# A hybrid decoder layer on one core: the conv layer norm, the first attention head, the second FFN norm and the seam of the FFN's two phases rearranged

## The chip, the cores and the metric

The kernel runs on one core of a Trainium2 chip. The core has TensorE (PE; its weight loads are shown as PEld), VectorE (DVE), ScalarE (ACT), GpSimd (POOL) and SyncE (SP), which issues nearly all DMA transfers here. The metric is the device time of one execution in microseconds (us).

## The reference

One decoder layer is computed for 1024 prompt tokens and for 8 sequences of 4 new tokens over 2048 cached positions, 1056 tokens in all, in float32:

- `h = rmsnorm(x) @ w_in`, split into a convolution input, latent queries, latent keys, a rotary key and two gates.
- Convolution branch: `u = a * sigmoid(g)`, a depthwise convolution of width 31 over 512 channels, then `y = silu(_layernorm(y, ln_g, ln_b))` with `_layernorm = (y - mean) * rsqrt(mean((y - mean)^2) + 1e-6) * g + b`, and `y @ w_conv_out`.
- Attention: 8 heads of 96 features, of which 32 are rotary; q and k of each head are RMS-normalised (`_head_norm`) before causal softmax attention. The sample tokens attend to a paged cache.
- `x = x + (sigmoid(g_conv) * conv + sigmoid(g_mla) * mla) @ w_out`, and at last the FFN, `x = x + (silu(h2 @ w_gate) * (h2 @ w_up)) @ w_down` with `h2 = rmsnorm(x)`, 1024 model features and 2816 hidden ones.

## The kernel before

**Arithmetic.** Each float32 operand of a large matmul is split into a rounded high part and a rest (`split`, L75 and L76: a cast on ACT, a subtraction on DVE or POOL), and each product takes three matmuls: high times high, rest times high, high times rest. Nearly all of them are recorded at L70.

**Conv layer norm.** The 1056 tokens are handled in three thirds `q` of 352 columns. `ln_mm` sums over the channels with a matmul by ones, `ln_b` subtracts the mean and squares, and `ln_c` (L416 to L431) works out `1/sqrt(v + eps)` as a full tile of 128 x 352: sqrt on ACT, reciprocal on DVE, one correction step. Then it multiplies `y`, applies silu (four channel blocks, L430) and splits the result into `cvh` and `cvl`, the operand of the `w_conv_out` product. Meanwhile PE computes the gates, `g()`: matmuls whose result ACT reads with a sigmoid into `sgo` (L345). Mean and variance are hung behind single gate tiles by `then=`.

**Attention.** Token blocks 0 to 7 get q and k (`qn`, `kn`) by `d_norm`, `d_post`. In `d_post` a block is multiplied by its reciprocal roots `r`: `qn` on DVE (L640), `kn` on POOL in two pieces (L644 and L646; the second piece of block 7 on DVE). Then the heads begin: `e_prep` transposes qn and kn of four blocks, splits them (qh, kh on ACT; ql, kl on DVE), and `e_score` makes a row block of scores in PSUM (`ps__...`, two banks), which DVE masks and minimises in one custom operation into `sm` (L867). The mask is set up by POOL (L786 to L788) and by ACT (L789).

**FFN norm.** The RMS norm of the last token block (`norm_a` to `norm_d`, L1460 to L1551) stands in line with the first FFN products, which `eight` and `go` place.

**FFN.** Both phases use seven products instead of eight (Strassen's scheme in 2 x 2 blocks; `ORDER` and `DORD` list the seven). Phase 1 has 11 strips `g`; each has a unit for the gate and one for the up projection (`unit`, L1725). A unit is 7 products x 2 column halves x 12 matmuls of 264 columns. The seven combinations of a finished strip go to DRAM (`td`, stores at L1637); `d_load` and `d_sums` read the strip's part of `w_down`, form four combinations on POOL and DVE and store them (`sd`, L1626 to L1634). Phase 2 has 14 rounds of 11 steps; a step is 12 matmuls and needs a right operand of `td` (`d_b`: load L1775, cast L1781, subtraction L1782) and, every second step, a strip of `w_down` or `sd` (`d_w`: load L1798 or L1800, cast L1810, subtraction L1811). Loads run four pieces ahead; there are three buffers for a split strip and 28 slots for right operands.

**What sets the order.** Each engine works through its instructions in the order of the program, after a scheduler with priorities (`tc.high_priority`) has placed them. SP issues the DMAs in order, too: a store that waits for its data holds up every load that stands behind it.

Of the kernel before, what the change touches and what calls it, by code (L numbers as in the profile page):

```python
# [44 lines left out]
def build(tc, a, o, upto="Z", dbg=None):  # L45
# [369 lines left out]

    def ln_c(q):  # L416
# [50 lines left out]
    g()  # L467
    w_c = [wload(wp, a["w_conv_out"][0, :, 0:2 * P], 4, 2 * P, G)]
# [19 lines left out]
    vhl = qkv.tile([P, 8, H, 2, DV], F32R, name="vhl")  # L488
    dq = pool("dq", side="right")
# [101 lines left out]
    def d_qk(i):  # L591
# [5 lines left out]
        if i < 8:  # L597
# [23 lines left out]
    def d_stats(j):  # L621
# [12 lines left out]
        V.scalar_tensor_tensor(out=r, in0=t, scalar=1.5, in1=r, op0=ALU.add, op1=ALU.mult)  # L634

    def d_post(i):
# [9 lines left out]
        (V if i == 7 else G).tensor_tensor(out=kn[:, i, :, DN:], in0=pe_all[:, i, :].unsqueeze(1).to_broadcast([P, H, DR]),  # L646
# [100 lines left out]
    d_post(6)  # L747
    d_post(7)
# [104 lines left out]
    def e_score(h, i):  # L853
# [4 lines left out]
        for g_ in range(i // 4 + 1):  # L858
# [8 lines left out]
        V.tensor_tensor_reduce(out=sm[:, :n], in0=ps_[:, :n], in1=mask[:, NP_ - n:], scale=1.0, scalar=BIG,  # L867
                               op0=ALU.add, op1=ALU.min, accum_out=st[:, 0:1])
# [839 lines left out]
    def unit(u, nxt, order):  # L1708
        for n_ in order:
# [7 lines left out]
            if u[0] == "u":  # L1717
# [47 lines left out]

    def d_b(n):

        for _ in range(n):
            if len(DB) == len(dbs):
                return  # L1770
            while len(dbt) < min(len(DB) + 4, len(dbs)):
                xi, k = dbs[len(dbt)]
                ts = [ctile(F32) for _ in range(2)]
                for q in range(2):
                    SP.dma_start(ts[q], td[DORD[xi] - 1, k, :, q * CQ:(q + 1) * CQ])  # L1775
                dbt.append(ts)
            x = dbs[len(DB)]
            hi, lo = slots[len(DB) % len(slots)]
# [8 lines left out]

    def d_w(n):

        while len(dwo) <= min(n, len(dws) - 1):  # L1790
            while len(dwr) < min(len(dwo) + 4, len(dws)):
                xi, p, kp = dws[len(dwr)]
                x, m = DORD[xi], min(2, NF2 - 2 * kp)
                w = rawtile()[:, 0:m * 2 * P]
                if x in (1, 2, 4):
                    j, i = {1: (0, 0), 2: (1, 0), 4: (1, 1)}[x]
                    c0 = (4 * i + 2 * p) * P
                    SP.dma_start(w.rearrange("p (e c) -> p e c", e=m), wdv[:, j, 2 * kp:2 * kp + m, c0:c0 + 2 * P])  # L1798
# [6 lines left out]
            if n_ >= len(dws) - 6:  # L1805

# [126 lines left out]
```

## Time and profile before

| | us |
|---|---|
| three runs | 1828.26, 1828.10, 1824.87; median 1828.1 |
| profiled execution | 1829.26 |
| its span (first to last instruction) | 1827.5 |
| PE busy in it | 1759.0 (96%) |
| DVE, ACT, POOL busy | 1252.3, 841.7, 769.8 |
| mean granted TensorE clock | 0.987 of full |

The span is the part of the execution that the profiler's records cover. An engine's busy share is an average over stages; the waits say which engine's work another one stood still for, and the windows give busy time, instruction counts, granted TensorE clock and DMA rate of a stretch.

### The profile page before, as it was taken

The page shows a single profiled execution, that of the slowest core. Times are in us where ns is not written, and L with a number is a line of the kernel's source. Part 1 is how long each engine was busy: PE and PEld are TensorE (multiplying, and loading weights), DVE is VectorE, ACT ScalarE, POOL GpSimd, SP SyncE. Part 2 cuts the span into 40 slices and gives each one's busy share as a digit, 9 for nine tenths or more (in the row PEclk, how much of TensorE's full clock was granted, in tenths as well). Part 3 has the DMA queues.
Part 4 walks back from the last instruction along what each step waited for, and adds up shares of the span by engine and source line. Part 5 has one row for each costly group of instructions (what it writes and reads, how often), then busy time and mean ns, then how long its engine had stood idle before and what let it go on. Part 6 is the DMA issues. An engine that isn't in the chain of part 4 may idle for free.

```text
span 1827.5 us, 34749 instructions
## 1 busy us (share of the span) xinstructions
PE 1759.0 (96%) x12932; PEld 1708.2 (93%) x12932; DVE 1252.3 (69%) x2437; ACT 841.7 (46%) x1892; POOL 769.8 (42%) x855
## 2 busy tenths in 40 slices
PE   8999999999899999999989999999999999799999
PEld 8999999989788899999979999999999999799998
DVE  5329999746788867666758689767676666666433
ACT  5311122554588867777763145332333333455332
POOL 2212112125655634343322047756555555665431
PEclk9999999999899999999999999999999999899999
DMA  6211222254000022121245210454445444887432
GB/s 209 63 52 48 71 84 94 82 178 123 1 30 12 2 88 70 59 82 53 93 146 174 82 30 27 145 152 150 149 154 161 140 145 148 250 247 232 146 96 93
DMA packets 197156, 199.15 MB, mean 109 GB/s; under 512 B 17400, under 2 KB 180516, under 8 KB 194931
## 3 DMA queue, kind: packets, MB, share of 16 engines
q1 hardware_dynamic: 194043, 178.05, 31.2%
q0 software_dynamic: 2944, 18.88, 3.1%
q8 instruction: 102, 1.67, 0.4%
q14 instruction: 67, 0.55, 0.1%
HBM read 145.87 MB, written 51.42 MB: 108 GB/s over the span
## 4 chain that ended last, share of the span: by engine, by line
PE 75%; DVE 9%; ACT 7%; DMA 3%; issue 3%; POOL 1%; SPq 1%; DVEq 0%; ACTq 0%; POOLq 0%
PE ps L70 51%; PE pp L70 6%; PE pd L70 3%; PE po L1117 2%; PE pq L70 2%; PE pt L891 1%; DMA c<-td 1%; PE ptc L1023 1%; PE po L905 1%; ACT pr L870 1%; ACT sqf L1043 1%; DVE b L1491 1%; PE pt L70 1%; PE pk L70 1%; DVE sm L867 1%
## 5 line engine op out<-in xcount | busy, mean ns | idle before, releaser
L70 PE MATMUL ps<-b,wh 128*128 128x264 f32 x3544 | 655.5, 287 | 14.3 <-ACT wh L1810 10.4
L70 PEld LDWEIGHTS ps<-b,wh 128*128 128x128 f32 x3544 | 552.9, 190 | 15.3 <-ACT wh L1810 10.7
L70 PE MATMUL ps<-b,wl 128*128 128x264 f32 x1772 | 503.9, 286 | 3.9 <-DVE wl L1811 3.0
L70 PEld LDWEIGHTS ps<-b,wl 128*128 128x128 f32 x1772 | 335.1, 190 | 5.5 <-DVE wl L1811 3.9
L1348 ACT CAST wh<-wr 128x512 fp32r<-128x512 f32 x157 | 97.1, 619 | 219.3 <-PE ps L70 180.4
L70 PE MATMUL ps<-hTh,wh 128*128 128x352 f32 x552 | 179.9, 326 | 0.0
L70 PE MATMUL ps<-hTl,wh 128*128 128x352 f32 x552 | 178.1, 323 | 0.0
L70 PE MATMUL ps<-hTh,wl 128*128 128x352 f32 x552 | 178.0, 322 | 0.0
L70 PE MATMUL pp<-panh,cTh 128*128 128x272 f32 x512 | 157.0, 307 | 8.0 <-DVE sraw L1044 6.5
L357 DVE SCALAR_TENSOR_TENSOR y<-up,cw,y 128x1024 f32<-128x1024 f32 x120 | 158.0, 1362 | 0.7
L986 POOL TENSOR_TENSOR cNl<-craw,cNh 128x256 fp32r<-128x256 f32 x128 | 88.7, 694 | 165.1 <-ACT cNh L985 165.0
L1349 POOL TENSOR_TENSOR wl<-wr,wh 128x512 fp32r<-128x512 f32 x78 | 105.3, 1350 | 110.3 <-ACT wh L1348 78.1
L70 PE MATMUL pp<-panh,cTl 128*128 128x272 f32 x512 | 149.2, 291 | 0.0
L70 PE MATMUL pp<-panl,cTh 128*128 128x272 f32 x512 | 147.8, 289 | 0.0
L70 PEld LDWEIGHTS pp<-panh,cTh 128*128 128x128 f32 x512 | 96.4, 188 | 12.3 <-DVE sraw L1044 10.2
L70 PEld LDWEIGHTS ps<-hTh,wh 128*128 128x128 f32 x552 | 103.7, 188 | 0.7
L70 PEld LDWEIGHTS ps<-hTl,wh 128*128 128x128 f32 x552 | 103.7, 188 | 0.6
L70 PEld LDWEIGHTS ps<-hTh,wl 128*128 128x128 f32 x552 | 103.7, 188 | 0.0
L872 POOL TENSOR_TENSOR pr<-pr,ste 128x128 f32<-128x128 f32 (+3 forms) x64 | 73.2, 1147 | 60.0 <-DVE ste L871 34.5
L76 POOL TENSOR_TENSOR wl<-wr,wh 128x1024 fp32r<-128x1024 f32 x13 | 37.7, 2902 | 142.2 <-ACT wh L75 142.2
L70 PEld LDWEIGHTS pp<-panl,cTh 128*128 128x128 f32 x512 | 96.9, 189 | 0.0
L1043 ACT ACTIVATE sqf<-pp 128x512 f32<-128x512 f32 x128 | 76.4, 597 | 44.2 <-ACT cTh L75 28.9
(888 smaller groups left out, 4361.5 us busy)
## 6 DMA issues: line engine op xcount, KB each, us to landing
td<-c SPq DMA_DIRECT2D x154, 132.0 KB
c<-td SPq DMA_DIRECT2D x154, 132.0 KB
wr<-in_w_in SPq DMA_DIRECT2D x24, 512.0 KB
wr<-in_w_gate SPq DMA_DIRECT2D x44, 256.0 KB
wr<-in_w_up SPq DMA_DIRECT2D x44, 256.0 KB
c<-in_w_down SPq DMA_DIRECT2D x88, 128.0 KB
sd<-c SPq DMA_DIRECT2D x88, 128.0 KB
wr<-sd SPq DMA_DIRECT2D x40, 256.0 KB
```

What stands on the lines that cost most here:

```text
L70: TE.matmul(out, l, r, start=first and i == 0, stop=last and i == n - 1)
L76: (eng or V).tensor_tensor(out=lo, in0=src, in1=f(hi), op=ALU.subtract)
L357: V.scalar_tensor_tensor(out=y[:, c, 0:NP_], in0=up[:, j:j + NP_], scalar=cw[:, c, j:j + 1], in1=y[:, c, 0:NP_], op0=ALU.mult, op1=ALU.add)
L867: V.tensor_tensor_reduce(out=sm[:, :n], in0=ps_[:, :n], in1=mask[:, NP_ - n:], scale=1.0, scalar=BIG, op0=ALU.add, op1=ALU.min, accum_out= ...
L870: at["ACT"] = S.activation(pr[:, :n], sm[:, :n], AF.Exp, scale=-1.0, bias=st[:, 0:1], accum_out=st[:, 1:2]).ins
L872: at["POOL"] = G.tensor_tensor(out=pr[:, :n], in0=pr[:, :n], in1=st[:, 2:3].to_broadcast([P, n]), op=ALU.mult).ins
L891: TE.transpose(pt[:, j, :], pr[:, (j0 + j) * P:(j0 + j + 1) * P], ident)
L986: G.tensor_tensor(out=nl[:, j], in0=craw[:, j], in1=f(nh[:, j, 0:KL]), op=ALU.subtract)
L1043: s["at"] = S.activation(sq, pp[:, :, wc], AF.Square).ins
L1117: TE.matmul(d, l, r, start=(pg == 0 and z == 0), stop=(pg == NPG and z == 1))
L1348: S.copy(h_, src[u][x][:, c])
L1349: eng.tensor_tensor(out=l_, in0=src[u][x][:, c], in1=f(h_), op=ALU.subtract)
```

## The change

- Conv layer norm: the variance is summed as 4 x 88 tokens on partitions (four matmuls by two columns of ones), its root is a power on POOL over 88 x 4 numbers, a copy on DVE spreads it over 128 columns, and four transposes on PE bring it back as rows. Silu becomes `z * sigmoid(z)`: sigmoid on ACT, `z` and the product on DVE. `ln_c` of a third is hung behind the next gate tile, and the split is made in halves. The split of the first `w_conv_out` strip moves from POOL to DVE.
- Attention: for blocks 6 and 7 the multiplications by the reciprocal roots move from before the first head to behind the first `sm`, in one 128 x 768 piece for kn as for qn. The reciprocal roots are kept in `csT`. The wide part of the mask is set after the operands of the first head.
- FFN norm: `norm_b(3)` moves behind two more `go`/`eight` pieces, `d_load(0, 0)` behind `norm_d(2, ...)`.
- FFN seam: in the last strip (`g` = 10) `d_load` and `d_sums` move from the up unit to the gate unit. The loads of the first five right operands are issued before the last unit (`d_bl(5)`), those of the first strips inside it (`d_wl`), and loading is separated from splitting. Split strips get nine buffers in place of three (six of the slots), right operands 22 slots in place of 28. In phase 2 strips are loaded eight ahead and split four ahead.

The core of the diff:

```diff
+    def ln_var(q):
+
+        pv = psb.tile([P, 512], F32, tag="s", name="ps", bufs=8)
+        for j in range(4):
+            TE.matmul(pv[:SUB, 2 * j:2 * j + 2], lns[q][:, j * SUB:(j + 1) * SUB], ones[:, 0:2], start=True, stop=True)
+        st = pb.tile([SUB, 2, 4], F32, tag="lnst", name="lnst", bufs=2)
+        V.tensor_scalar(out=st[:, 0], in0=pv[:SUB, 0:8].rearrange("p (j z) -> p j z", z=2)[:, :, 0], scalar1=EPS, scalar2=None, op0=ALU.add)
+        G.tensor_tensor(out=st[:, 1], in0=st[:, 0], in1=nhalf[:SUB, 0:4], op=ALU.pow)
+        lnp[q] = pb.tile([SUB, 4, P], F32, tag="lnrb", name="lnrb", bufs=1)
+        V.tensor_copy(lnp[q], st[:, 1].unsqueeze(2).to_broadcast([SUB, 4, P]))
+
     def ln_c(q):
         cs = slice(q * CH, (q + 1) * CH)
-        v = pb.tile([P, CH], F32, tag="sg", name="sg", bufs=2)
-        V.tensor_scalar(out=v, in0=lnp[q][:, :CH], scalar1=EPS, scalar2=None, op0=ALU.add)
-        r = pb.tile([P, CH], F32, tag="rq_r", name="rq_r", bufs=1)
-        t = pb.tile([P, CH], F32, tag="rq_t", name="rq_t", bufs=1)
-        S.activation(t, v, AF.Sqrt)
-        V.reciprocal(r, t)
-        V.tensor_tensor(t, r, r, ALU.mult)
-        V.tensor_tensor(t, t, v, ALU.mult)
-        V.tensor_scalar(out=t, in0=t, scalar1=-0.5, scalar2=1.5, op0=ALU.mult, op1=ALU.add)
-        V.tensor_tensor(r, r, t, ALU.mult)
-        V.tensor_tensor(y[:, :, cs], y[:, :, cs], r.unsqueeze(1).to_broadcast([P, 4, CH]), ALU.mult)
-        for c in range(4):
-            S.activation(y[:, c, cs], y[:, c, cs], AF.Silu, scale=gsm[:, 4 + c:5 + c], bias=gsm[:, 8 + c:9 + c])
-        split(cvh[:, :, cs], cvl[:, :, cs], y[:, :, cs])
+        pr = psb.tile([P, 512], F32, tag="s", name="ps", bufs=8)
+        for j in range(4):
+            TE.transpose(pr[:, j * SUB:(j + 1) * SUB], lnp[q][:, j], ident[:SUB, :SUB])
+        V.tensor_tensor(y[:, :, cs], y[:, :, cs], pr[:, :CH].unsqueeze(1).to_broadcast([P, 4, CH]), ALU.mult)
+
+        for c2 in range(2):
+            sz = pb.tile([P, 2, CH], F32, tag="up", name="sz", bufs=2)
+            for c in (2 * c2, 2 * c2 + 1):
+                g_, b_ = gsm[:, 4 + c:5 + c], gsm[:, 8 + c:9 + c]
+                S.activation(sz[:, c % 2], y[:, c, cs], AF.Sigmoid, scale=g_, bias=b_)
+                V.tensor_scalar(out=y[:, c, cs], in0=y[:, c, cs], scalar1=g_, scalar2=b_, op0=ALU.mult, op1=ALU.add)
+            ys = y[:, 2 * c2:2 * c2 + 2, cs]
+            V.tensor_tensor(ys, ys, sz, ALU.mult)
+            split(cvh[:, 2 * c2:2 * c2 + 2, cs], cvl[:, 2 * c2:2 * c2 + 2, cs], ys)
...
     def var(q):
-        ln_mm(q)
-        ln_c(q)
+        ln_var(q)
+        if q:
+            ln_c(q - 1)
 
     g(then=mean)
     g(then=var)
-    g()
-    w_c = [wload(wp, a["w_conv_out"][0, :, 0:2 * P], 4, 2 * P, G)]
+    g(then=lambda q: q == 0 and ln_c(2))
+    w_c = [wload(wp, a["w_conv_out"][0, :, 0:2 * P], 4, 2 * P)]
...
+            if i > 5:
+                G.tensor_copy(kn[:, i, :, DN:], pe_all[:, i, :].unsqueeze(1).to_broadcast([P, H, DR]))
...
+        S.activation(mask[:, 0:NP_ - P].rearrange("p (j q) -> p j q", j=7), ident.unsqueeze(1).to_broadcast([P, 7, P]), AF.Copy, scale=0.0)
         for n_ in range(AH):
             e_score(*flat[n_])
+        at0 = at["DVE"]
+        for i in (6, 7):
+            for eng, t, w in ((V, qn, 0), (G, kn, 1)):
+                with tc.issue_after(at0):
+                    eng.tensor_tensor(out=t[:, i], in0=t[:, i], in1=rr3[:, w, i % 2].unsqueeze(2).to_broadcast([P, H, DH]), op=ALU.mult)
...
-            if u[0] == "u":
+            if nxt is None:
+
+                d_b({1: 2, 6: 4, 2: 5, 7: 5, 5: 7, 4: 7, 3: 7}[n_])
+                if n_ == 7:
+                    d_bl(7, tmp)
+                d_wl({7: 2, 5: 4, 4: 6}.get(n_, 0))
+                d_w({4: 1, 3: 2}.get(n_, 0))
+            elif u == ("g", NF2 - 1):
+                if n_ in (1, 6):
+                    d_load(u[1], n_ // 6)
+                if n_ in (2, 7):
+                    d_sums(u[1], n_ // 7)
+            elif u[0] == "u":
                 if n_ in (2, 4):
                     d_load(u[1], n_ // 4)
                 if n_ in (5, 3):
                     d_sums(u[1], (5, 3).index(n_))
-            if nxt is None:
-                d_b(2 if n_ != 3 else 1)
...
     norm_b(3)
-    go(nc_, 1)
-    for x in ((1,), (2,)):
-        for q in range(2):
-            eight(q, 1, x)
+    for q in range(2):
+        eight(q, 1, (2,))
...
+    def d_bl(n, get=lambda: ctile(F32)):
+
+        while len(dbt) < min(n, len(dbs)):
+            xi, k = dbs[len(dbt)]
+            ts = [get() for _ in range(2)]
+            for q in range(2):
+                SP.dma_start(ts[q], td[DORD[xi] - 1, k, :, q * CQ:(q + 1) * CQ])
+            dbt.append(ts)
...
+        while len(DB) < min(n, len(dbs)):
+            x, ts = dbs[len(DB)], dbt[len(DB)]
+            hi, lo = slots[len(DB) % 22]
...
-            if n_ >= len(dws) - 6:
-
-                hi, lo = [t[:, 0:m] for t in slots[(7 * NF2 + n_ - len(dws) + 6) % len(slots)]]
-            else:
-                hi, lo = [t[:, 0:m] for t in whl()]
+            hi, lo = [t[:, 0:m] for t in (whl() if n_ % 9 < 3 else slots[22 + n_ % 9 - 3])]
...
+        if g_ + 1 == NF2:
+            d_bl(5)
         unit(("u", g_), ("g", g_ + 1) if g_ + 1 < NF2 else None, ORDER)
...
+                d_wl(len(dws))
...
-                d_w(6 * t + k // 2 + 2)
-                if (11 * p + k) % 2 == 0 and (xi or p or k > 2):
-                    d_b(1)
+                n_ = 6 * t + k // 2
+                d_wl(n_ + 8)
+                d_w(n_ + 4)
+                n_ = 11 * xi + (11 * p + k) // 2 + 8
+                d_bl(n_ + 4)
+                d_b(n_)
```

The order of the instructions moves as follows. The first place is SP's queue at the end of phase 1: `td` stores are those of a strip's combinations, `wr<-in_w_down` are strips for phase 2, `c<-td` right operands for it. Before (these stand behind the last strip's results):

```order
L1637 DMA td_74<-c_18855 128x264
L1637 DMA td_74<-c_18976 128x264
L1634 DMA sd_75<-c_19325 128x256
L1634 DMA sd_75<-c_19329 128x256
L1634 DMA sd_75<-c_19331 128x256
L1634 DMA sd_75<-c_19327 128x256
L1775 DMA c_19403<-td_74 128x264
L1775 DMA c_19404<-td_74 128x264
L1798 DMA wr_19425<-in_w_down 128x2x256
L1798 DMA wr_19431<-in_w_down 128x2x256
L1798 DMA wr_19437<-in_w_down 128x256
```

After (the `td` stores here are those of strip 9; the ones of strip 10 begin 16 rows below the last one shown; line numbers in rows of after are those of the changed kernel):

```order
L1659 DMA td_74<-c_18439 128x264
L1659 DMA td_74<-c_18455 128x264
L1322 DMA wr_18919<-in_w_up 128x4x128
L1831 DMA wr_19262<-in_w_down 128x2x256
L1831 DMA wr_19264<-in_w_down 128x2x256
L1805 DMA u2_12372<-td_74 128x264
L1805 DMA u3_12373<-td_74 128x264
L1831 DMA wr_19312<-in_w_down 128x2x256
L1805 DMA c_19086<-td_74 128x264
L1805 DMA c_19087<-td_74 128x264
L1805 DMA c_19090<-td_74 128x264
```

The last load of `in_w_up` and the first strips and right operands now stand together, ahead of all stores of strip 10. Before, the fourth to sixth strip stood behind them and behind the `sd` stores.

The second place is POOL at the start of attention, where the mask and kn of blocks 6 and 7 meet. Before:

```order
L644 TENSOR_TENSOR kn_3520<-kn_3520,std_4485 128x8x64
L646 TENSOR_TENSOR kn_3520<-pe_all_82,std_4485 128x8x32
L644 TENSOR_TENSOR kn_3520<-kn_3520,std_4485 128x8x64
L787 MEMSET mask_4667 128x128
L882 MEMSET PTh_4772 128x128
L883 MEMSET PTl_4773 128x128
L788 AFFINE_SELECT mask_4667<-mask_4667 128x128
```

After:

```order
L803 MEMSET mask_4702 128x128
L940 TENSOR_TENSOR kn_3559<-kn_3559,csT_67 128x768 x2
L898 MEMSET PTh_4811 128x128
L899 MEMSET PTl_4812 128x128
L804 AFFINE_SELECT mask_4702<-mask_4702 128x128
```

The copies of the rotary part of kn are made earlier; two multiplications of 128 x 768 stand between the mask's two instructions. On DVE, at the same place, before:

```order
L640 TENSOR_TENSOR qn_3519<-qn_3519,std_4485 128x768 x2
L646 TENSOR_TENSOR kn_3520<-pe_all_82,std_4485 128x8x32
L848 SCALAR_TENSOR_TENSOR ql_4674<-pt_4675,gqT_68,qh_4673 96x512
L76 TENSOR_TENSOR kl_4683<-pt_4684,kh_4682 96x512
L867 ISA sm_4696,ste_4695<-ps__4691,mask_4667 128x128
```

After:

```order
L652 SCALAR_TENSOR_TENSOR csT_67<-std_4524 128x32
L863 SCALAR_TENSOR_TENSOR ql_4708<-pt_4709,gqT_68,qh_4707 96x512
L76 TENSOR_TENSOR kl_4717<-pt_4718,kh_4716 96x512
L882 ISA sm_4731,ste_4730<-ps__4726,mask_4702 128x128
L882 ISA ste_4730 128x1
L940 TENSOR_TENSOR qn_3558<-qn_3558,csT_67 128x768 x2
L882 ISA sm_4742,ste_4741<-ps__4737,mask_4702 128x256
```

ql and kl of the first head come directly behind the reciprocal roots (`csT`), and the two multiplications of qn stand between the first `sm` and the second.

The third place is ACT at the end of the conv layer norm (third `q` = 2). Before:

```order
L75 CAST wh_3420<-wr_3418 128x1024
L345 ACT_TABLE_LOAD
L345 ACTIVATE sgo_3338<-ps_3391 128x352
L345 ACTIVATE sgo_3424<-ps_3425 128x352
L430 ACT_TABLE_LOAD
L430 ACTIVATE y_1203<-y_1203,gsm_65 128x352 x4
L75 CAST cvh_1195<-y_1203 128x4x352
L345 ACT_TABLE_LOAD
L345 ACTIVATE sgo_3424<-ps_3451 128x352
```

After:

```order
L440 ACTIVATE sz_3388<-y_1203,gsm_65 128x352 x2
L75 CAST cvh_1195<-y_1203 128x2x352
L440 ACTIVATE sz_3396<-y_1203,gsm_65 128x352 x2
L75 CAST wh_3459<-wr_3457 128x1024
L345 ACTIVATE sgo_3355<-ps_3430 128x352
L75 CAST cvh_1195<-y_1203 128x2x352
L345 ACTIVATE sgo_3463<-ps_3464 128x352
L75 CAST cvh_1195<-y_1203 128x2x352
L345 ACTIVATE sgo_3463<-ps_3490 128x352
```

The table loads are gone; sigmoids, halves of the cast and gate reads follow each other.

## Rows read from the trace of the kernel before

**Rows 1.** The page: busy time, share of the span, instructions

```profile
PE 1759.0 (96%) x12932; PEld 1708.2 (93%) x12932; DVE 1252.3 (69%) x2437; ACT 841.7 (46%) x1892; POOL 769.8 (42%) x855
```

**Rows 2.** PE's waits: us in total, times, longest

```profile
PE ps L70 <- ACT wh L1810: 10.4, 1, 10.4
...
PE ps L70 <- ACT sgo L345: 4.4, 1, 4.4
...
PE ps L70 <- DVE b L1551: 3.2, 1, 3.2
PE ps__4691 L863 <- DVE kl L76: 3.1, 1, 3.1
PE ps L70 <- DVE wl L1811: 3.0, 2, 1.9
PE ps L1469 <- DVE u L1460: 2.9, 2, 2.6
```

**Rows 3.** The page: DMA issues, KB each

```profile
c<-td SPq DMA_DIRECT2D x154, 132.0 KB
...
wr<-sd SPq DMA_DIRECT2D x40, 256.0 KB
```

**Rows 4.** Phase 2, windows: us, PE PEld DVE ACT POOL busy (x), PEclk, DMA share, GB/s

```profile
1590.00:1594.00 4.00, 2.39 (x11) 2.39 (x12) 0.89 (x1) 1.54 (x3) 2.64 (x3) 0.50 0.95 295
1594.00:1597.00 3.00, 3.00 (x24) 3.00 (x24) 0.87 (x2) 1.60 (x4) 1.31 (x3) 0.90 1.10 360
1629.00:1632.00 3.00, 3.00 (x16) 3.00 (x15) 2.26 (x5) 0.54 (x2) 1.32 (x2) 0.50 0.89 255
1760.00:1780.00 20.00, 20.00 (x168) 20.00 (x167) 6.66 (x15) 4.66 (x9) 3.70 (x4) 1.00 0.36 99
```

**Rows 5.** SP's queue ahead of PE's longest stop: start, us, work

```profile
1578.87 5.40 SPq L1637 DMA_DIRECT2D td<-c  x8
1584.33 1.91 SPq L1634 DMA_DIRECT2D sd<-c  x4
...
1587.27 2.44 SPq L1798 DMA_DIRECT2D wr<-in_w_down  x5
```

**Rows 6.** Windows at the end of the conv norm, columns as in rows 4

```profile
382.50:390.00 7.50, 6.32 (x22) 6.33 (x23) 2.30 (x5) 4.15 (x10) 2.36 (x1) 0.54 0.43 150
390.00:412.00 22.00, 22.00 (x141) 22.00 (x140) 8.08 (x19) 6.29 (x14) 7.77 (x7) 1.00 0.85 271
```

**Rows 7.** ACT ahead of the gate that PE waits for, timeline

```profile
378.06 2.40 ACT L430 ACTIVATE y<-y,gsm 128x352 f32<-128x352 f32 x4 [1.62 <-DVE y L428]
380.48 1.36 ACT L75 CAST cvh<-y 128x1408 fp32r<-128x1408 f32 x1
381.87 1.28 ACT L345 ACT_TABLE_LOAD   x1
```

**Rows 8.** ACT over the conv norm, groups by line

```profile
L345 ACT ACT_TABLE_LOAD x6 | 7.7, 1283 | 0.1
```

**Rows 9.** POOL in the last FFN norm: the power, group by line

```profile
L1472 POOL TENSOR_TENSOR nst<-nst,nhalf 88x3 f32<-88x3 f32 x1 | 1.0, 1039 | 0.0
```

**Rows 10.** DVE at the first head, timeline

```profile
491.32 2.67 DVE L640 TENSOR_TENSOR qn<-qn,std 128x768 f32<-128x768 f32 x2
...
495.34 0.67 DVE L76 TENSOR_TENSOR kl<-pt,kh 96x512 fp32r<-96x512 f32 x1
496.91 0.29 DVE L867 CUSTOM_DVE_ANT_0 sm<-ps__4691,mask 128x128 f32<-128x128 f32 x1 [0.90 <-PE ps__4691 L864]
```

**Rows 11.** POOL at the first head, timeline

```profile
491.37 1.81 POOL L644 TENSOR_TENSOR kn<-kn,std 128x512 f32<-128x512 f32 x1 [1.92 <-DVE std L634]
...
494.44 1.22 POOL L644 TENSOR_TENSOR kn<-kn,std 128x512 f32<-128x512 f32 x1
...
496.05 0.29 POOL L788 TENSOR_SCALAR_AFFINE_SELECT mask<-mask 128x128 f32<-128x128 f32 x1
```

**Rows 12.** Window in the last FFN norm, columns as in rows 4

```profile
1152.50:1155.00 2.50, 0.15 (x1) 0.15 (x1) 2.50 (x5) 0.93 (x2) 2.50 (x3) 0.86 0.32 105
```

More of the change, by code (lines that the diff above doesn't have):

```diff
@@ L414, in ln_b @@
         ln_add(q, [sqa[:, 0], sqa[:, 1], sqb[:, 0], sqb[:, 1]])
+    SUB = 88
+    def ln_var(q):
[7 more added lines that the diff above has]
+        V.tensor_copy(lnp[q], st[:, 1].unsqueeze(2).to_broadcast([SUB, 4, P]))
@@ L488, in build @@
     vhl = qkv.tile([P, 8, H, 2, DV], F32R, name="vhl")
+    rr3 = csT[:, 0].rearrange("p (w z h) -> p w z h", w=2, z=2)
     dq = pool("dq", side="right")
@@ L633, in d_stats @@
         V.tensor_tensor(t, t, v, ALU.mult)
-        V.scalar_tensor_tensor(out=r, in0=t, scalar=1.5, in1=r, op0=ALU.add, op1=ALU.mult)
+        V.scalar_tensor_tensor(out=rr3 if j == 3 else r, in0=t, scalar=1.5, in1=r, op0=ALU.add, op1=ALU.mult)
     def d_post(i):
@@ L645, in d_post @@
                         in1=r[1].unsqueeze(2).to_broadcast([P, H, DN]), op=ALU.mult)
-        (V if i == 7 else G).tensor_tensor(out=kn[:, i, :, DN:], in0=pe_all[:, i, :].unsqueeze(1).to_broadcast([P, H, DR]),
+        G.tensor_tensor(out=kn[:, i, :, DN:], in0=pe_all[:, i, :].unsqueeze(1).to_broadcast([P, H, DR]),
                         in1=r[1].unsqueeze(2).to_broadcast([P, H, DR]), op=ALU.mult)
@@ L866, in e_score @@
         sm = pe_.tile([P, NP_], F32, tag="sm", name="sm", bufs=2)
-        V.tensor_tensor_reduce(out=sm[:, :n], in0=ps_[:, :n], in1=mask[:, NP_ - n:], scale=1.0, scalar=BIG,
-                               op0=ALU.add, op1=ALU.min, accum_out=st[:, 0:1])
+        x = V.tensor_tensor_reduce(out=sm[:, :n], in0=ps_[:, :n], in1=mask[:, NP_ - n:], scale=1.0, scalar=BIG,
+                                   op0=ALU.add, op1=ALU.min, accum_out=st[:, 0:1])
+        at.setdefault("DVE", x.ins)
         pr = pe_.tile([P, NP_], F32, tag="pr", name="pr", bufs=5)
@@ L1728, in build @@
             eight(q, 0, x)
+    go(nc_, 1)
+    for q in range(2):
+        eight(q, 1, (1,))
     norm_b(3)
-    go(nc_, 1)
-    for x in ((1,), (2,)):
-        for q in range(2):
-            eight(q, 1, x)
+    for q in range(2):
+        eight(q, 1, (2,))
     nc_ = norm_c(3)
@@ L1750, in build @@
     raw(("g", 1))
-    d_load(0, 0)
     for m in range(4):
         norm_d(2, m)
+    d_load(0, 0)
     if stop("G"):
@@ L1764, in build @@
     dbt = []
-    def d_b(n):
[L1768 to L1778, printed above, removed]
+    def d_bl(n, get=lambda: ctile(F32)):
+        while len(dbt) < min(n, len(dbs)):
+            xi, k = dbs[len(dbt)]
+            ts = [get() for _ in range(2)]
+            for q in range(2):
+                SP.dma_start(ts[q], td[DORD[xi] - 1, k, :, q * CQ:(q + 1) * CQ])
+            dbt.append(ts)
+    def d_b(n):
+        while len(DB) < min(n, len(dbs)):
+            x, ts = dbs[len(DB)], dbt[len(DB)]
+            hi, lo = slots[len(DB) % 22]
             for q in range(2):
                 qs_ = slice(q * CQ, (q + 1) * CQ)
-                S.copy(hi[:, qs_], dbt[len(DB)][q])
-                (V, G)[q].tensor_tensor(out=lo[:, qs_], in0=dbt[len(DB)][q], in1=f(hi[:, qs_]), op=ALU.subtract)
+                S.copy(hi[:, qs_], ts[q])
+                (V, G)[q].tensor_tensor(out=lo[:, qs_], in0=ts[q], in1=f(hi[:, qs_]), op=ALU.subtract)
             DB[x] = (hi, lo)
@@ L1786, in build, with d_wl @@
     dwr, dwo = [], []
-    def d_w(n):
[L1790 to L1798, printed above, removed]
-                else:
-                    SP.dma_start(w, sd[{5: 0, 6: 1, 7: 2, 3: 3}[x], p, kp, :, 0:m * 2 * P])
-                dwr.append(w)
+    def d_wl(n):
+        while len(dwr) < min(n, len(dws)):
+            xi, p, kp = dws[len(dwr)]
+            x, m = DORD[xi], min(2, NF2 - 2 * kp)
+            w = rawtile()[:, 0:m * 2 * P]
+            if x in (1, 2, 4):
+                j, i = {1: (0, 0), 2: (1, 0), 4: (1, 1)}[x]
+                c0 = (4 * i + 2 * p) * P
+                SP.dma_start(w.rearrange("p (e c) -> p e c", e=m), wdv[:, j, 2 * kp:2 * kp + m, c0:c0 + 2 * P])
+            else:
+                SP.dma_start(w, sd[{5: 0, 6: 1, 7: 2, 3: 3}[x], p, kp, :, 0:m * 2 * P])
+            dwr.append(w)
+    def d_w(n):
+        while len(dwo) < min(n, len(dws)):
             n_ = len(dwo)
@@ L1846, in d_add @@
             V.tensor_tensor(xT[:, mo, cs], xT[:, mo, cs], pt[:, :CQ], ALU.subtract if x == 4 else ALU.add)
-    d_w(1)
     for xi, x in enumerate(DORD):
```

4 lines of the change are left out of this document (removed).

## The prediction

> **What bounds the kernel now.** I read first the page's engine line [rows 1]: PE is busy for 1759.0 of 1827.5 us. So some 68 us of PE's idle time are all that a rearrangement can take out, plus what PE loses at half clock behind a stop. Then the waits of PE, longest first [rows 2]: the reader is to see that the change's four places are all in this list. The FFN seam holds 10.4 (wh, L1810) and 3.0 (wl, L1811); the conv norm 4.4 (sgo, L345); the last FFN norm 3.2 (b, L1551) and the larger part of 2.9 (u, L1460); the first head 3.1 (kl). Last the windows around them, for the clock and for whoever is late there. The sum is made on the profiled execution, 1829.26 us (its span and 1.76 around it), which is 1.2 above the median of the three runs, 1828.1; I take the change of the one off the other.
>
> **FFN seam.** Before PE's long stop SP spends 5.40 us on eight stores of strip 10, each behind its combination, then 1.91 on four stores of sums; only at 1587.27 does it issue the fourth strip of `w_down` [rows 5], which in the queue stands behind both. PE starts again on the cast of that strip. In the changed order the first strips and operands are issued ahead of all stores of strip 10, and the sums of that strip are made a unit earlier. That removes:
> - the long stop, 10.4, and the two waits for wl, 3.0, which fall in the catching up behind it [rows 2];
> - half clock. At full pace 168 matmuls take 20.00 us, 0.119 each [rows 4]. In the 4 us from 1590 PE did 11 in 2.39 us at clock 0.50, for which 1.31 would do: 1.1 lost. In the 3 us from 1629 it did 16 in 3.00 at 0.50, for 1.9: 1.1 lost [rows 4].
>
> Together 15.6; shorter waits there are further down the same list, and I don't count them. What could be late next is the DMA. An operand (2 x 132 KB) and a strip (256 KB) [rows 3] each feed 24 matmuls, since an operand serves two rounds and a strip two steps: 520 KB per 24 x 0.119 = 2.86 us, about 180 GB/s. While catching up the queue moved 295 and 360 GB/s [rows 4], so phase 2 itself is fed with room to spare. The unit before it is tight: ahead of phase 2 there are 8 strips and some 16 operands to move, 2.1 + 4.2 MB, about 21 us at 300 GB/s, and the unit has 168 matmuls, 20 us. But the first operands are loaded before that unit, and only the first third must have landed when it ends. The moved `d_load` and `d_sums` bring no new work, only the same 8 loads, 8 additions and 8 stores about 20 us earlier. I take 15 of the 15.6. Bounds: 5 if loads are still late, 17 if the shorter waits go too.
>
> **Conv layer norm.** ACT is late here. Ahead of the gate read that PE waits for it does four silus (2.40), a cast (1.36) and a table load (1.28) [rows 7]; six such loads stand ahead of gate reads alone, 7.7 us [rows 8], and as many ahead of sqrt and silu. PE stops for 4.4 [rows 2] and then runs at clock 0.54: 22 matmuls in 6.32 us [rows 6], where by 141 in 22.00 [rows 6] they take 3.43, so 2.9 are lost. In the changed order sigmoid alternates with sigmoid, sqrt is gone, so are the loads, and the last third's `ln_c` is hung a gate tile earlier. So I take both away, 7.3. Against it: PE's three variance matmuls by ones, over 352 columns each, become 12 small ones and 12 transposes, and the transposes of a third wait for POOL's power and for DVE's copy; a wait there hits PE in its own queue. The nearest row for the power is that of the FFN norm, 1.04 [rows 9]. I price the exchange of matmuls at nothing and such waits at 0.8 in all, about one power that is not hidden; the bounds are 0 and 3.1, all three. DVE gains the products `z * sigmoid(z)` and loses three reciprocals and three correction chains; where PE is slowed it is busy for 2.30 of 7.50 us [rows 6], which leaves room for the difference. Result: 6.5 gained, bounds 4.2 to 7.3.
>
> **First head.** Before, DVE does qn twice (2.67) and kn once ahead of ql and kl, so kl ends at 496.0; the first `sm` then starts at 496.91 [rows 10]. Now ql and kl are early and PE's wait of 3.1 [rows 2] is nearly gone. But the first `sm` needs the mask also, and POOL's instruction for it, at 496.05 before, now stands behind two multiplications of 128 x 768. For 128 x 512 POOL took 1.22 beside ql and kl, and 1.81 beside DVE's qn [rows 11]; for 768 columns that is 1.83 or 2.72, so two end 3.7 or 5.4 after 491.4, and with 0.7 for the small instructions the mask is there at 495.8 or 497.6. So the first `sm` is between 1.1 earlier and 0.7 later than before. Behind it DVE does qn twice, 2.67, ahead of the second `sm`; PE has two score banks and can't go on with the fourth score until that second `sm` has read its bank. That wait for kl is thus replaced by one for the mask and one for the second `sm`, which comes at 498.5 to 500.7. By PE's queue (two scores left at half clock) that is between 0.5 gained and 2.7 lost. I take 0.5 lost, near the first end, because DVE's qn no longer falls beside POOL's kn.
>
> Rows 11 show that the same multiplication took half as long again beside DVE's qn, which has two inputs in SBUF, as beside ql and kl, which read PSUM. The Trainium skill, SBUF — State Buffer, section "Who interferes with whom", says that a DVE instruction with two SBUF inputs holds up a GpSimd instruction that reads SBUF and that the second one blocks fully, while one that has a single SBUF input does not. These rows agree that only qn disturbs, but show less than a full block: 1.81, not 1.22 and one qn on top. By the rule as written the mask would come at 495.8 here, since nothing but ql and kl runs beside kn, the early end of the bounds.
>
> **Last FFN norm.** Moving `norm_b(3)` behind 24 matmuls lets PE go on where it waited up to 2.6 for `u` (L1460) [rows 2]. But DVE is what is full: in the window of the largest stop there, 1152.5 to 1155, it is busy for 2.50 of 2.50 while PE does one matmul [rows 12]. DVE's work is not less, so the time that PE wins at 1112 it waits again at 1155. I take 0.5 gained, bounds 0 and 2.5.
>
> **Sum.** 15 + 6.5 - 0.5 + 0.5 = 21.5 gained. 1829.26 - 21.5 = 1807.8 for the profiled execution; against the median 1806.6. I say 1806.5.
>
> **The rivals.**
> 1. The loads are still late at the seam: the queue must carry the last weights of phase 1, the stores of strip 10 and the first 16 operands within one unit (21 us of transfers against 20 by the sum above). PE then stops for about half as long as before, with its half clock of 1.1 again. For it: a DMA share of 0.95 and 1.10 behind the old stop [rows 4]. Against it: that was a backlog after the stop. 8 of 15 come back: 1814.5. Chance 0.2.
> 2. The conv norm's gain is eaten: PE stands at the transposes of each third as long as it did at the gate. For it: three engines in a chain (POOL, DVE, PE) where before PE only waited for ACT. Against it: a gate tile lies between. 5 of 6.5 lost: 1811.5. Chance 0.1.
> 3. More comes off: the small waits at the seam and the 2.5 of the norm go as well, and the head costs nothing: 17 + 7.3 + 2.5 = 26.8, so 1801.3. Chance 0.13.
> 4. Slower: strip 10 starves in phase 1. The last `in_w_up` load now stands behind eight stores of strip 9's combinations in SP's queue. As at the old seam, SP would sit about 5.4 in them, and that load's cast and split come behind; PE then stops for 10.4 within the last unit with 1.1 of half clock, and because the strips stand behind that load, the old stop of 10.4 and the waits of 3.0 at phase 2 remain. 11.5 more, less 6.5 of the conv norm: 1833.1. It decides if PE idles over 7 us within the last two units. Against it: these stores' data is made a whole unit earlier, while SP has no waits to speak of. Chance 0.04.
>
> The forecast has the other 0.53, with a range of its own of 1803 to 1810.
>
> **How the numbers follow.** A change of less than 0.2%, 3.7 us, can't be told from none here. Forecast and rivals 1 to 3 are all faster by more than that, 0.96; of that I put 0.03 to a mixture of 1 and 2 that ends within 0.2%. So faster 0.93, same 0.03, slower 0.04. The range goes from 1798, all bounds at their best (17 + 7.3 + 0.5 + 2.5 = 27.3 gives 1800.8, and the runs' own spread of 3.4 below that), to 1817, which takes in rival 1 with its worst conv norm.
>
> **What would show it.** In the profile of the changed kernel: right, if the wait for wh of L1810's successor is gone from PE's list or below 1 us, and the windows around the end of phase 1 show PE full at clock 1.0; if no gate read is in the list any more and the clock stays at 1.0 behind it; if the first head has lost kl as PE's releaser and gained `sm`; and if the last norm still stops PE for `b` near 1150. Wrong, if PE's idle time at the FFN seam is above 4 us, or stands in the last unit of phase 1, or if transposes in the conv norm wait above 1 us each.

## The result and the profile after

The changed kernel takes 1815.8 us (median of four runs, 1814.55 to 1817.43) against 1828.2 for the kernel before (again the median of four, 1824.87 to 1828.91): a ratio of 0.9936, interval 0.9919 to 0.9954, 12.4 us faster. The forecast was 1806.5 with a range from 1798 to 1817: right in direction and within the range, but with little more than half of the 21.5 us, and outside the 1803 to 1810 that the forecast has as its own. The span of the profiled execution is 1813.7, that of before was 1827.5, and the mean granted clock is 0.991 in place of 0.987.

PE's waits after (us in total, times, longest; to be held against [rows 2]):

```profile
PE ps L70 <- DVE b L1573: 4.3, 1, 4.3
...
PE ps L70 <- DVE wl L1844: 4.1, 2, 3.5
...
PE ps L70 <- DVE wl L1371: 3.5, 2, 2.5
PE ps L70 <- DVE nst L1493: 2.9, 1, 2.9
...
PE ps__4748 L877 <- DVE ste L882: 1.4, 1, 1.4
...
PE ps L433 <- DVE lnrb L427: 1.0, 1, 1.0
PE ps L70 <- POOL wl L1844: 0.9, 1, 0.9
```

The three largest waits that the change was aimed at are gone: wh of the FFN seam (10.4), the gate read of the conv norm (4.4) and, but for a little, kl of the first head (3.1). In their places stand a subtraction of the FFN seam (wl L1844, 4.1 and 0.9), the small wait for `lnrb` and a wait for the second `sm` (`ste` L882). The norm has 4.3, 2.9 and 2.5 in place of 3.2, 2.6 and 1.7.

The windows after that answer to [rows 4] and [rows 6] (columns as there):

```profile
382.50:390.00 7.50, 7.50 (x48) 7.50 (x47) 4.94 (x13) 3.38 (x10) 0.65 (x1) 1.00 0.84 290
390.00:412.00 22.00, 22.00 (x141) 22.00 (x140) 6.99 (x16) 5.16 (x9) 10.81 (x8) 1.00 0.87 263
1570.00:1580.00 10.00, 6.62 (x50) 6.19 (x50) 9.97 (x19) 7.03 (x17) 8.00 (x8) 1.00 0.78 233
1580.00:1585.00 5.00, 3.74 (x22) 3.75 (x23) 5.00 (x6) 1.46 (x4) 5.00 (x5) 0.78 0.61 184
```

At the end of the conv norm PE runs through at clock 1.00: 48 matmuls in 7.50 us where there were 22 in 6.32. At the FFN seam it is busy for 6.62 of 10 us, while DVE is busy for 9.97: here is what the forecast missed.

**Where the time went, by stretches.** The same PE instruction was looked up in each kernel's timeline; the table gives the time between two of them, for the kernels before and after and for those of the experiments below. The marks are the last matmul of the `w_conv_out` product, the first 128-column product with the values (`po`, in the first head), the first position product of the cached rows (`ptp`), the first 264-column merge product, the last of the FFN's first strip that the norm holds up (`ps<-b,wh`), and the last transpose of the output.

```
kernel      to conv  first  attention  cache and   FFN    FFN phase 1
            product  head   (rest)     merge       norm   from there, phase 2
before       430.3   83.3    137.1      403.6      107.6      661.4
after        425.3   82.9    139.4      402.4      109.2      650.0
only_conv    424.9   83.1    137.0      402.2      108.2      657.9
only_head    429.9   81.1    137.4      407.1      108.3      658.9
only_norm    429.6   82.9    137.1      404.1      109.0      658.3
only_seam    429.9   83.0    137.2      406.4      107.7      652.6
fix_seam     425.3   83.3    138.4      403.4      107.6      645.2
no_norm      425.0   83.8    138.4      403.1      107.9      650.7
fix_head     425.6   81.0    137.3      402.4      108.6      650.8
best         425.5   80.2    137.3      403.2      109.0      645.1
```

A column shows what an edit does in its place, and how much the place varies where nothing is edited: 402.2 to 407.1 in the fourth, where nothing was changed at all. Most of that spread is the clock: the waits of PE there are the same ones (2.6 for `phl`, 1.1 for `mx`, 0.9 for `ath` and so on), and what differs is how long half clock follows on them; the mean granted clock of the stretch is 0.99 in the kernel with 402.2 and 0.97 in the one with 407.1. All six kernels with the conv part are at the low end, at 402.2 to 403.4, and the four without it at 403.6 to 407.1, so a hand of that part can't be excluded. Each row is one execution, the profiled one: that of only_seam was the slowest of its four (1822.59, the others 1818.1 to 1819.2).

### The profile page after: what moved, and what is told of

Its sections match the earlier page's. It is cut to its first block, busy times and chain, and to the rows that moved or that the text cites. A ratio compares the mean times of both kernels' runs of the same rounds, so it can differ in the third digit from the quotient of the medians.

```text
span 1813.7 us, 34862 instructions
## 1 busy us (share of the span) xinstructions
PE 1753.4 (97%) x12962; PEld 1704.4 (94%) x12962; DVE 1256.8 (69%) x2446; ACT 821.8 (45%) x1880; POOL 767.9 (42%) x858
## 4 chain that ended last, share of the span: by engine, by line
PE 77%; DVE 9%; ACT 6%; issue 3%; DMA 3%; POOL 1%; SPq 1%; DVEq 0%; ACTq 0%; POOLq 0%
PE ps L70 53%; PE pp L70 6%; PE pd L70 3%; PE po L1139 2%; PE pq L70 2%; PE pt L907 1%; PE po L921 1%; PE ptc L1045 1%; ACT pr L886 1%; DVE b L1513 1%; ACT sqf L1065 1%; PE pt L70 1%; DVE sm L882 1%; ACT cTh L75 1%; PE pk L70 1%
## 5 line engine op out<-in xcount | busy, mean ns | idle before, releaser
L70 PE MATMUL ps<-b,wh 128*128 128x264 f32 x2840 | 523.1, 286 | 5.6 <-DVE b L1573 4.3
L70 PEld LDWEIGHTS ps<-b,wh 128*128 128x128 f32 x2840 | 441.7, 189 | 6.3 <-DVE b L1573 4.5
L70 PE MATMUL ps<-b,wl 128*128 128x264 f32 x1420 | 404.2, 285 | 8.5 <-DVE wl L1844 4.1
L70 PEld LDWEIGHTS ps<-b,wl 128*128 128x128 f32 x1420 | 268.2, 189 | 9.6 <-DVE wl L1844 4.5
L70 PE MATMUL ps<-b,b 128*128 128x264 f32 x1284 | 163.4, 286 | 2.9 <-DVE nst L1493 2.9
L70 PEld LDWEIGHTS ps<-b,b 128*128 128x128 f32 x1284 | 158.8, 189 | 3.2 <-DVE nst L1493 3.2
```

What stands on the lines that cost most here:

```text
L70: TE.matmul(out, l, r, start=first and i == 0, stop=last and i == n - 1)
```

## The experiments

Two series. The first puts each of the four places alone into the kernel before; the second changes the changed kernel, at one place each, and then at three.

**only_seam**: before, with the part of the diff from `unit` on that concerns `d_b`, `d_w`, `d_load` and `d_sums`.

```diff
-            if nxt is None:
-                d_b(2 if n_ != 3 else 1)
+            if nxt is None:
+                d_b({1: 2, 6: 4, 2: 5, 7: 5, 5: 7, 4: 7, 3: 7}[n_])
...
+    def d_wl(n):
...
+        if g_ + 1 == NF2:
+            d_bl(5)
...
```

> The kernel before with the change of the FFN seam alone. Theory A (DMA order: once the first strips and operands stand ahead of strip 10's stores in SP's queue, PE no longer waits for a load): as in the whole change, about 11.3 us faster, and what is left of PE's stops at the start of phase 2 (about 5 us with half clock) ends with a subtraction on DVE or POOL, not a load. Theory B (the seam's gain in the whole change is partly the other places' doing, since they shift the loads): clearly less than 11, below 8.

Measured: 1818.85 against 1827.31, ratio 0.995 (0.9933 to 0.9966), 8.5 us faster; the interval, 6.2 to 12.2, takes in the figures of both theories. Its PE waits from 1560 to 1600:

```profile
PE ps L70 <- DVE wl L1821: 3.3, 2, 2.9
PE ps L70 <- ACT wh L1820: 1.5, 1, 1.5
PE ps L70 <- POOL wl L1821: 0.9, 1, 0.9
```

5.7 us of stops are left (5.0 in the changed kernel), which end with subtractions and one cast. The table shows why less than the 11.4 that the traces of before and after give: the other kernels with the old seam take 657.9 to 658.9 in the last column, the profiled execution of before 661.4. Its catching up was a longer one (3.7 us of waits behind the long stop and half clock again, [rows 2, 4]; 2.0 to 2.5 in the others). Against these three the changed kernel's 650.0 is about 8 less. This kernel's own 652.6 belongs to its slowest execution, with 6.8 us of half clock behind the stops where the changed kernel has 3.4. So the seam is worth about 8, and theory A holds for the kind of wait that is left.

**only_conv**: before, with `ln_var`, the new `ln_c`, their places behind the gates and the split of the first `w_conv_out` strip on DVE.

```diff
     def var(q):
-        ln_mm(q)
-        ln_c(q)
+        ln_var(q)
+        if q:
+            ln_c(q - 1)
...
```

> The kernel before with the conv layer norm alone. By the offsets of PE's instructions between the two traces the place gave 7.3 behind the gate and took 2.4 ahead of it, in the second and third third of the gates: net 4.9 faster. If the 2.4 belongs to something else, the net is 6.5 to 7.3.

Measured: 1820.76 against 1827.31, ratio 0.9963 (0.995 to 0.9975), 6.5 us faster (4.6 to 9.1). At the place the six kernels with it have 424.9 to 425.6 and the four without 429.6 to 430.3: 4.7 between their means, and nothing else was edited ahead of that mark. Where the rest of the 6.5 lies is not shown; the stretch of the cache and the merge, where the half clock comes and goes, would be a place for it, and the interval takes in 4.7 alone. PE's groups by line from 331 to the first `w_conv_out` matmul, after:

```profile
L402 PE MATMUL ps<-s,ones 128*128 128x352 f32 x6 | 2.3, 458 | 0.0
L422 PE MATMUL ps<-ones,s 128*88 128x2 f32 x24 | 2.1, 211 | 0.0
L433 PE MATMUL ps<-ident,lnrb 88*128 88x88 f32 x12 | 1.5, 247 | 1.0 <-DVE lnrb L427 1.0
```

and of before:

```profile
L402 PE MATMUL ps<-s,ones 128*128 128x352 f32 x12 | 4.5, 458 | 0.0
```

Up to the first matmul on `cvh` (377.2 before, 379.5 after) the place costs 2.3: the wait of 1.0 for the third `lnrb`, and, as the rest, 1.3 by PE's own instructions, 36 short ones for 6 long ones. From there to the last matmul it gives 7.3, as the forecast had it. Whether PE's stop went because the table loads are gone, or because `ln_c` now stands a gate tile earlier, no run here separates.

**only_norm**: before, with `norm_b(3)` and `d_load(0, 0)` moved.

```diff
-    norm_b(3)
     go(nc_, 1)
-    for x in ((1,), (2,)):
-        for q in range(2):
-            eight(q, 1, x)
+    for q in range(2):
+        eight(q, 1, (1,))
+    norm_b(3)
+    for q in range(2):
+        eight(q, 1, (2,))
...
```

> The kernel before with the moved norm_b(3) and d_load(0, 0) alone. Theory A (DVE is full there, and the norm's later steps now come later, so their three waits add up to more): 1.6 us slower, waits for nst and wl in place of that for u. Theory B (the 1.6 is from the place in time, or noise): within 0.5 of before.

Measured: 1827.44 against 1827.31, ratio 1.0001 (0.9991 to 1.001): no difference. Its waits in the norm:

```profile
PE ps L70 <- DVE b L1551: 4.3, 1, 4.3
PE ps L70 <- DVE nst L1471: 3.0, 1, 3.0
PE ps L70 <- DVE wl L1349: 2.5, 1, 2.5
PE ps L70 <- POOL b L1491: 1.2, 1, 1.2
```

The 2.6 for `u` is gone, and 3.0 for `nst`, 2.5 for `wl` and 1.1 more for `b` have come. Theory A has the waits right. But the column of the norm runs from 107.6 to 109.0 without the move and from 107.6 to 109.2 with it, so its 1.6 of the one pair of traces is within what the place varies by. It is worth nothing that these runs can tell.

**only_head**: before, with the reciprocal roots in `csT` and the multiplications of blocks 6 and 7 behind the first `sm`.

```diff
-    d_post(6)
-    d_post(7)
...
+        at0 = at["DVE"]
+        for i in (6, 7):
+            for eng, t, w in ((V, qn, 0), (G, kn, 1)):
+                with tc.issue_after(at0):
...
```

> The kernel before with the first attention head alone. Theory A: 0.4 faster up to the first transposes of the probabilities; the later 2.4 in mid-attention are one late load of wukr (5.0 against 3.7 us) with half clock behind it and not the change, so they come or stay away by chance: total between 0.4 faster and 2 slower, and the wait for PTl is long only where that load is slow. Theory B: the 2.4 are the change's: 2 us slower in each execution with a normal load.

Measured: 1826.5 against 1827.31, ratio 0.9996 (0.9986 to 1.0006): no difference that can be told, the interval goes from 2.6 faster to 1.1 slower. At the place it is 2 us faster (81.1 against 83); in the whole change the same edit gives nothing (82.9, 83.3 and 83.8 in the three kernels with it and the conv norm). DVE's timeline shows one difference, here in the kernel with this part alone:

```profile
494.49 0.29 DVE L868 CUSTOM_DVE_ANT_0 sm<-ps__4687,mask 128x128 f32<-128x128 f32 x1 [1.79 <-POOL mask L790]
494.71 0.08 DVE L868 DVE_READ_ACCUMULATOR2_ANT ste<- 128x1 f32 x1
494.71 0.95 DVE L926 TENSOR_TENSOR qn<-qn,csT 128x768 f32<-128x768 f32 x1
495.58 0.42 DVE L868 CUSTOM_DVE_ANT_0 sm<-ps__4698,mask 128x256 f32<-128x256 f32 x1
```

and in the changed kernel:

```profile
487.80 0.68 DVE L76 TENSOR_TENSOR kl<-pt,kh 96x512 fp32r<-96x512 f32 x1
490.27 0.29 DVE L882 CUSTOM_DVE_ANT_0 sm<-ps__4726,mask 128x128 f32<-128x128 f32 x1 [1.80 <-POOL mask L804]
490.49 0.08 DVE L882 DVE_READ_ACCUMULATOR2_ANT ste<- 128x1 f32 x1
490.49 1.82 DVE L940 TENSOR_TENSOR qn<-qn,csT 128x768 f32<-128x768 f32 x2
492.23 0.42 DVE L882 CUSTOM_DVE_ANT_0 sm<-ps__4737,mask 128x256 f32<-128x256 f32 x1
```

The scheduler put one multiplication of qn ahead of the second `sm` in the one and two in the other; both wait 1.8 for the mask. Another is the clock. PE's idle time in the column of the first head is 6.0 us in only_conv, 4.9 to 5.5 in the three (the changed kernel, fix_seam and no_norm) and 4.1 in only_head; but fix_seam and no_norm lie at half clock there for 10.2 us, the other three for 6.8.

Of the later 2.4 in mid-attention there is nothing here (137.4). Theory A holds there: in the trace after ACT waits for the load of `wukr`,

```profile
590.49 1.05 ACT L837 CAST panh<-wukr 128x1024 fp32r<-128x1024 f32 x1 [2.06 <-DMA wukr<-in_w_uk]
```

and PE 2.2 behind it; in the nine other traces that wait is 0.7 to 0.8. fix_seam and no_norm lost 1.4 in the same stretch without it: their clock is at 0.66 from 560 to 565, while only_conv and fix_head, with the same waits from 510 to 600 (2.1 for `ql`, of which 1.1 at once, 0.9 to 1.0 for `PTl`, 0.8 for `kh`), stay at 1.00. Why it falls in the one and not in the other is open.

**fix_seam**: the changed kernel, with another use of the buffers at the seam. In the changed kernel the first three split strips lie in the rotating buffers and the next six in the slots that hold operands of phase 1's last two products; now the first six lie in the slots that phase 1 leaves first, and are split within its last unit.

```diff
-            hi, lo = slots[len(DB) % 22]
+            hi, lo = slots[6 + len(DB) % 22]
...
-            hi, lo = [t[:, 0:m] for t in (whl() if n_ % 9 < 3 else slots[22 + n_ % 9 - 3])]
+            hi, lo = [t[:, 0:m] for t in (slots[n_ % 9] if n_ % 9 < 6 else whl())]
...
-                d_b({1: 2, 6: 4, 2: 5, 7: 5, 5: 7, 4: 7, 3: 7}[n_])
+                d_wl({1: 2, 6: 2, 2: 3, 7: 4, 5: 5, 4: 6, 3: 7}[n_])
+                d_w({1: 1, 6: 2, 2: 2, 7: 3, 5: 4, 4: 4, 3: 5}[n_])
+                d_b({1: 0, 6: 2, 2: 4, 7: 5, 5: 7, 4: 7, 3: 7}[n_])
                 if n_ == 7:
                     d_bl(7, tmp)
-                d_wl({7: 2, 5: 4, 4: 6}.get(n_, 0))
-                d_w({4: 1, 3: 2}.get(n_, 0))
```

> The changed kernel with another assignment of buffers at the FFN seam: the first six split strips lie in the slots that are free first (operands of phase 1's products 1 and 6), the right operands in the other 22, and the first five strips are split within the last unit of phase 1. Theory A (what is left of PE's stops there, 5.0 us and half clock, is the third strip's subtraction, which had to wait for a buffer of the last unit and then stood behind later strips on DVE): these waits fall below 1 us, 4 to 6 us faster than the changed kernel, about 1811. Theory B (DVE is full in these 15 us, so the sum of its work sets the end): the waits move into the last unit or to another subtraction, within 1.5 us of the changed kernel.

Measured: 1809.88 us (1808.89 to 1811.2), ratio to before 0.9905 (0.9889 to 0.9922): 5.9 below the changed kernel (the two intervals just touch, but all runs of the one lie below all runs of the other), and 4.8 to 5.6 less in the last column than the three kernels with the changed seam and conv norm. The changed kernel's DVE at the seam shows what was late (start, us; the third strip's subtraction is the last row, PE starts 0.1 behind its end):

```profile
1574.55 0.99 DVE L1844 TENSOR_TENSOR b<-wr,b 128x512 fp32r<-128x512 f32 x1
...
1577.27 1.75 DVE L1844 TENSOR_TENSOR b<-wr,b 128x512 fp32r<-128x512 f32 x1
...
1579.97 1.23 DVE L1844 TENSOR_TENSOR wl<-wr,wh 128x512 fp32r<-128x512 f32 x1
```

The two rows ahead are splits of later strips, into slots (`b`), while the strip that PE waits for has `wl`, a rotating buffer. In fix_seam the first three subtractions are long done when phase 2 begins; two of them are on DVE:

```profile
1551.81 0.69 DVE L1844 TENSOR_TENSOR b<-wr,b 128x512 fp32r<-128x512 f32 x1 [1.20 <-ACT b L1843]
1552.86 1.35 DVE L1844 TENSOR_TENSOR b<-wr,b 128x512 fp32r<-128x512 f32 x1 [0.36 <-ACT b L1843]
```

and PE's windows across the seam are full (columns as in rows 4), although DVE is as full as before:

```profile
1565.00:1575.00 10.00, 9.73 (x80) 9.74 (x81) 9.97 (x19) 5.92 (x16) 9.47 (x11) 1.00 0.76 224
1575.00:1585.00 10.00, 10.00 (x85) 10.00 (x84) 5.66 (x12) 3.41 (x8) 7.62 (x9) 1.00 0.81 237
```

Theory A, then: it was the order of the splits and the buffers behind it, not the sum of DVE's work. The edit changes the two together, and splits five strips within the last unit where the changed kernel's program has two; which of these counts is not separated.

**no_norm**: the changed kernel, with the norm's order of before (the diff of only_norm, reversed).

> The changed kernel with the last FFN norm's order of before. Theory A (the moved norm_b costs 1.4 to 1.6 us at its place): 1.5 us faster than the changed kernel, about 1814. Theory B (later stages give it back, as the kernel with this part alone was level with before): level.

Measured: 1814.17 us (1812.94 to 1817.1), ratio to before 0.9929 (0.991 to 0.9947), against 0.9936 (0.9919 to 0.9954) for the changed kernel. The intervals lie over each other, and the norm's column is 107.9 against 109.2: theory B, or too small to be told.

**fix_head**: the changed kernel, with POOL's select of the mask ahead of kn, and qn behind the second `sm`.

```diff
...
-        at0 = at["DVE"]
         for i in (6, 7):
             for eng, t, w in ((V, qn, 0), (G, kn, 1)):
-                with tc.issue_after(at0):
+                with tc.issue_after(at_m.ins if w else at["sm"][1]):
...
```

> The changed kernel with the mask's select on POOL ahead of kn's two multiplications, and qn's two multiplications on DVE behind the second sm. Theory A (after kl, the mask behind 2.9 us of kn and then qn ahead of the second sm hold PE): the waits of PE for DVE's ste (1.4 and 0.8) go, 2 to 3 us faster at the place; the sum of 1.5 to 3 faster. Theory B (qn and kn of these blocks are needed right behind the scores, so PE waits for them instead): 0 to 0.5.

Measured: 1812.34 us (1811.25 to 1818.58), ratio to before 0.9928 (0.9904 to 0.9952). By the medians that is 3.5 below the changed kernel, but the intervals lie over each other. At the place it is 1.9 faster (81.0 against 82.9), and both waits for `ste` are gone. That agrees with theory A at the place; the total is not told apart from that of the changed kernel.

**best**: the three together.

> The three together: buffers of the FFN seam, order of the first head, the norm's order of before. If each of them is worth what theory A says (5, 2 and 1.5), about 1807.5; if only the seam is, about 1811.

Measured: 1805.51 us (1804.25 to 1806.26), ratio to before 0.9877 (0.9861 to 0.9894), 21.5 us faster than before and 10.3 than the changed kernel, whose interval lies wholly above this one. That is 2 less than the expected 1807.5. It is chance that the 21.5 are also the forecast's: this kernel has another seam, another head and no moved norm. In the first head its DVE does not wait for the mask any more and starts the second `sm` 0.4 behind the first; POOL does the mask before the roots are there, and then kn:

```profile
485.05 0.29 POOL L804 TENSOR_SCALAR_AFFINE_SELECT mask<-mask 128x128 f32<-128x128 f32 x1
486.59 2.90 POOL L939 TENSOR_TENSOR kn<-kn,csT 128x768 f32<-128x768 f32 x2 [1.25 <-DVE csT L652]
```

## Why the prediction was right in direction and too high

**The figure.** The time lies within the range only because the range was drawn to take in rival 1, whose 1814.5 is the nearest of the recorded figures. But rival 1 is not what happened: it has PE stand still for late loads, and none of the changed kernel's stops at the seam ends with a load or a cast. That the time lies in the range is in part luck.

**FFN seam, forecast 15, about 8.** By the prediction's own sign it was wrong here: "PE's idle time at the FFN seam is above 4 us", and it was 5.0. What it said of the queue was right: with the loads ahead of strip 10's stores, no wait of PE for a load's cast is left in the changed kernel. The step that failed is "What could be late next is the DMA": it did not ask for the buffer into which a strip is split, nor for the order in which DVE splits. (ACT does wait for right operands, 13.4 us in nine waits between 1560 and 1592, but no stop of PE ends there.) The rotating buffer of the third strip was held by phase 1's last product, until 1569, and then other splits came first: the strip's cast starts at 1576.20, its subtraction at 1579.97, behind two later strips on DVE. 5.0 us of stops with their half clock came of it, and fix_seam took 4.8 to 5.9 away. The second part of the gap is the sum's other end: the last stretch of the one execution that was profiled was 2.5 to 3.5 longer than in the other three traces with the old seam. Its waits behind the long stop were longer, and the second of the two 1.1 is in none of the three. 13.2 were there to be had (best, 645.1, against the middle of those three, 658.3).

**Conv norm, forecast 6.5, 4.7 at its place.** The 7.3 came as worked out. The exchange of PE's matmuls, taken at nothing, cost 1.3, and the wait behind the chain of POOL and DVE 1.0, for 0.8 taken. The kernel with this part alone is faster by 6.5, so its size as a whole can't be said closer than 4.7 to 6.5.

**First head, forecast 0.5 lost, nothing at its place.** The wait for kl was replaced by those for the mask and for the second `sm`, as the forecast had it. The mask was there earlier than its lower bound, since the two multiplications of kn took 2.90 and not 3.7. With nothing beside them that reads two operands from SBUF they ran undisturbed, as the rule of the Trainium skill has it (SBUF — State Buffer, "Who interferes with whom"). The row that the prediction scaled up for this, 1.22 for 512 columns "beside ql and kl", was not undisturbed: it starts at 494.44, and until 494.75 DVE was still in its own product for kn, with two operands in SBUF. The last section shows that this row and the 1.81 both tell of a full block, where the prediction read less than one. Further on, the two products of qn took 1.82 and not 2.67, again with nothing of POOL's beside them; and the late end for the second `sm` should read 500.3 by the prediction's own terms (497.6 + 2.67), not 500.7.

**FFN norm, forecast 0.5, nothing.** "The time that PE wins at 1112 it waits again at 1155" is what the waits show.

**Not in the sum:** mid-attention and the stretch behind it, where single executions differ by 1 to 3 us by half clock and one late load. The forecast took a term from one trace for what each execution has.

## What to carry to other kernels

When a queue's order is the wait, also follow the buffers into which the freed loads go, and the order in which an engine fills them: the first piece that is needed belongs into the room that becomes free first. A gain that is read off one trace holds, behind its longest stop, a share that belongs to that execution; the same stretch in a second trace tells how much. And where instructions are set behind an anchor, set each one behind the instruction that it must not delay, not all behind the first. Before a row is taken as an instruction's undisturbed time, look at what the other engine was doing when it began.

## What the runs showed of the hardware

The same DVE instruction, a product of two SBUF operands of 128 x 704, took 0.89 us alone and 2.55 while POOL subtracted two SBUF operands of 128 x 1024. Both kinds stand in the timeline of the best kernel's conv norm, DVE and then POOL:

```profile
353.86 0.89 DVE L443 TENSOR_TENSOR y<-y,sz 128x704 f32<-128x704 f32 x1
...
357.01 2.55 DVE L443 TENSOR_TENSOR y<-y,sz 128x704 f32<-128x704 f32 x1
```

```profile
356.40 2.42 POOL L76 TENSOR_TENSOR wl<-wr,wh 128x1024 fp32r<-128x1024 f32 x1
```

DVE's instruction ends 0.74 us behind POOL's, its own 0.89 less 0.15: it was held until POOL was done. The five other such products of this conv norm took 0.88 to 0.89. The third `lnrb`, for which PE waits 1.0, stands right behind this product; whether that wait goes when POOL's subtraction is moved was not tried.

The same shows in the kernel before, where POOL's kn [rows 11] meets DVE's products. DVE and then POOL:

```profile
448.10 1.83 DVE L640 TENSOR_TENSOR qn<-qn,std 128x768 f32<-128x768 f32 x1
...
491.32 0.96 DVE L640 TENSOR_TENSOR qn<-qn,std 128x768 f32<-128x768 f32 x1
...
493.92 0.83 DVE L646 TENSOR_TENSOR kn<-pe_all,std 128x256 f32<-128x256 f32 x1
```

```profile
448.08 1.05 POOL L644 TENSOR_TENSOR kn<-kn,std 128x512 f32<-128x512 f32 x1 [0.65 <-DVE std L634]
```

At 448 POOL starts first and takes 1.05, and DVE's qn, 0.02 later, takes 1.83. At 491 DVE starts first and takes 0.96, and POOL's kn takes 1.81: it ends 0.90 behind DVE's product, its own 1.05 less 0.15. The one of 1.22, at 494.44, also ends 0.90 behind DVE's product (494.75). In these rows the instruction that comes second is held until the first is done, and the time that it is held stands in its own duration and not as idle time of its engine.
